# Attention stage of a two-layer trunk on one core: norm and first queries ahead of the values' products, scores with turned sign, small sums moved between engines

## The chip, the core and the metric

The kernel runs on one core of a Trainium2 chip. A core has five engines with a queue of instructions each, worked through in order: TensorE (PE in the rows; its weight loads are PEld) multiplies matrices into PSUM, VectorE (DVE) and ScalarE (ACT) do elementwise work, GpSimd (POOL) too, and SyncE (SP) issues DMA transfers. They meet only at semaphores. The metric is the device time of one execution in microseconds, the median of three runs.

## What is computed

The input is one sequence of 512 tokens with 1024 channels in float32. Layer 0 mixes by causal pooling, layer 1 by attention over a window of 128 tokens; each is followed by a gated MLP with a short convolution. The change touches the attention of layer 1 alone:

```python
qkv = h @ w_qkv + b_qkv                       # h = rms_norm(x, g); 16 query heads, 4 key/value heads of 64
scores = einsum(q, k_band) * 64**-0.5         # 4 blocks of 128 queries, each against 256 keys
scores = where(mask, scores - slope[head] * dist, -inf)
m = maximum(max(scores, -1), sink[head])
p = exp(scores - m)
denom = sum(p, -1) + exp(sink[head] - m)
o = einsum(p / denom, v_band)
return o @ w_o
```

## The kernel before

Activations lie with channels on the partitions: eight tiles `h[c]` of 128 channels by 512 tokens. Every product in float32 is made of three passes (`mm3`, lines 84 to 86): each operand is split into a high and a low part, and high by high, high by low and low by high are added in PSUM. So each 128 by 1024 weight tile takes one ScalarE instruction for the high part (line 98) and one subtraction for the low part (line 99), on VectorE or on GpSimd as the caller says; `proj` asks for GpSimd. The high and low tiles rotate through four buffers, so the split of a tile waits for the last product with the tile four before it; the raw tiles rotate through three.

The RMS norm is folded in late. The products use `h` scaled by the norm's weights only. `norm1.stats` sums squares over channels with four tiny matmuls (line 230), a chain of small VectorE instructions makes the reciprocal root (`rsqrt_mean`, lines 190 to 204), and `norm1.spread` spreads it over the partitions (VectorE line 240, four matmuls line 241, one ScalarE copy, line 244). Keys, queries and values are multiplied by it (`rb`, or `r` per token) when they leave PSUM.

The attention stage starts with three groups of products: keys (`kps`, weight tiles kq0 and kq1, 48 matmuls of 512 columns), values (`vps`, 96 of 256 columns), and the eight query chunks (weight tiles kq2 to kq9, 24 of 512 columns each; chunk c makes `q[c]`). `queries(c, ps)` takes a chunk out of PSUM: a product with `rb` on VectorE (line 451), scale and bias on ScalarE (452), then for each half a copy on ScalarE (458) and a subtraction on VectorE (459). `keys(n)` does the like for a key head.

Then come 16 units, one for each key head n and block b. `scores(n, b)` makes 8 score matmuls of 256 columns (line 540) and four VectorE instructions (543), which add the ALiBi distance and accumulate the row maximum into `neg`; then VectorE turns the sign of `neg` (554) and forms `es` (555), ScalarE takes the exponential of `es` (556) and of the four heads with the row sums (559), VectorE adds the denominator and inverts it (560, 561), and GpSimd scales the four heads (563). Two units later `transposed` turns them (571) and splits them (574, 575), three units later `weighted` multiplies them by the values (12 matmuls of 256 columns) and splits the result into `oh` and `ol` (590, 591).

Between them `fill(upto, have)` puts other TensorE work: one step is three matmuls of 512 columns, first of the remaining query chunks, then of the output projection with `w_o`. `RATE` says how many steps go to one unit. The program's order is what the author writes, but a scheduler below the language may let instructions of one engine pass each other, so the order on each engine is shown from the built program. PSUM has eight banks, here in four rings: t (banks 6, 7), s (2, 3, 4), pj (5, 0) and av (1).

Of the kernel before, what the change touches and what calls it, by code (L numbers as in the profile page):

```python
# [22 lines left out]
AF = mybir.ActivationFunctionType  # L23
# [4 lines left out]
D = 1024  # L28
# [29 lines left out]
def trunk(ctx: ExitStack, tc: tile.TileContext, x_tok, x_t, vecs, w_pool, w_kq, w_v, w_o, w_in, w_out, out_a, out_b):  # L58
# [18 lines left out]
    def bank(tag):  # L77
        rings[tag].append(rings[tag].pop(0))
        return banks[rings[tag][-1]]
# [13 lines left out]
    def weights(src, n, name, eng=None, raw=None):  # L93

        raw = raw or fetch(src, n, name)
        h = wp.tile([P, 1024], F32R, tag="wh", name=f"{name}_h")
        l = wp.tile([P, 1024], F32R, tag="wl", name=f"{name}_l")
        A.activation(h[:, :n], raw[:, :n], AF.Copy)  # L98
        (eng or V).tensor_tensor(l[:, :n], raw[:, :n], h[:, :n].bitcast(F32), ALU.subtract)  # L99
        return h, l  # L100
# [282 lines left out]
    with tc.tile_pool(name="ap", bufs=2) as ap:  # L383
# [16 lines left out]
        for t in (vh, vl):  # L400
            G.memset(t.bitcast(F32), 0.0)

        def proj(i, ps, ks=range(NC), w=None):
            w = w or weights(w_kq[i], D, f"kq{i}", G)
            for k in ks:
                mm3(ps, part(w, k), xs1[k], k == 0, k == NC - 1)
            return w


        qps = bank("pj")  # L410
        vps = [bank("s") for a in range(2)]
        ssp = bank("av")
        kps = [bank("t") for c in range(2)]
        kw = [weights(w_kq[i], D, f"kq{i}") for i in range(2)]
        wv = [weights(w_v[:, a * 1024 : (a + 1) * 1024], 1024, f"wv{a}") for a in range(2)]
        for k in range(NC):
            for c in range(2):
                proj(c, kps[c], [k], kw[c])
        for j in range(NT):
            for k in range(NC):  # L420
                xk = tuple(t[:, j * P : (j + 1) * P] for t in xs1[k])
                wk = part(wv[k // 4], k % 4, 256)
                mm3(vps[j // 2][:, (j % 2) * 256 : (j % 2 + 1) * 256], xk, wk, k == 0, k == NC - 1)
        r = norm1.stats(ssp)
        proj(2, qps)
        rb = norm1.spread(bank("s"), r)

        ku = []
        for c in range(2):
# [32 lines left out]

        key = {0: keys(0)}
        q = {0: queries(0, qps)}
        for j in range(NT):
            ps = vps[j // 2][:, (j % 2) * 256 : (j % 2 + 1) * 256]
            vv = ap.tile([P, 256], F32, tag="vv", name=f"vv{j}", bufs=1)
            V.scalar_tensor_tensor(vv, ps, r[:, j : j + 1], vec[:, V_BV : V_BV + 256], ALU.mult, ALU.add)
            dh, dl = (t[:, j, : 8 * HD].rearrange("p (n z d) -> p n z d", n=4, z=2)[:, :, 1, :] for t in (vh, vl))
            v4 = vv.rearrange("p (n d) -> p n d", n=4)  # L470
            A.activation(dh, v4, AF.Copy)
            V.tensor_tensor(dl, v4, dh.bitcast(F32), ALU.subtract)  # L472
        oh = ap.tile([P, NC, S], F32R, name="oh", bufs=1)
        ol = ap.tile([P, NC, S], F32R, name="ol", bufs=1)

# [24 lines left out]

        def work():

            for c in range(1, NC):
                for _ in fill_q(c):
                    yield 0
            for m, ks in ((0, range(4)), (1, range(4)), (0, range(4, 6)), (1, range(4, 6))):
                yield 2 * ks.stop
                for _ in fill_wo(m, "pj", ks):
                    yield 2 * ks.stop
            for m in range(2, 4):  # L510
                yield NU
                for _ in fill_wo(m, "s", range(6)):
                    yield NU
# [11 lines left out]
        def scores(n, b):  # L525
            w = P if b == 0 else 2 * P
            neg = small(ap, 4, 32, tag="neg", name=f"neg{n}{b}", bufs=3)
            den = small(ap, 4, 16, tag="den", name=f"den{n}{b}", bufs=3)
            es = small(ap, 4, 16, tag="es", name=f"es{n}{b}", bufs=3)
            sink = vec[:, V_SINK + 4 * n : V_SINK + 4 * n + 4]  # L530
            kk = max(b - 1, 0) * P
            sc = []
            for pr in range(2):
                ps = bank("s")
                st = ap.tile([P, 2, 2 * P], F32, tag="sc", name=f"sc{n}{b}{pr}", bufs=6)
                for par in range(2):
                    o = ps[:, par * 256 : par * 256 + 256]
                    qt = q[2 * n + pr][par][:, b * P : (b + 1) * P]
                    for x, kt in enumerate(key[n]):
                        T.matmul(o, lhsT=qt, rhs=kt[:, kk : kk + 256], start=x == 0, stop=x == 1)  # L540
                for par in range(2):
                    i = 2 * pr + par
                    V.tensor_tensor_reduce(  # L543
                        out=st[:, par, :w],
                        in0=ps[:, par * 256 : par * 256 + w],
                        in1=dist[:, 2 * P - w :],
                        scale=slopes[4 * n + i],
                        scalar=sink[:, i : i + 1],
                        op0=ALU.add,
                        op1=ALU.max,  # L550
                        accum_out=neg[:, i : i + 1],
                    )
                sc.append(st)
            V.tensor_scalar(neg, neg, -1.0, None, ALU.mult)
            V.tensor_tensor(es, neg, sink, ALU.add)
            A.activation(es, es, AF.Exp)
            heads = [sc[i // 2][:, i % 2, :w] for i in range(4)]
            for i, t in enumerate(heads):
                A.activation(t, t, AF.Exp, bias=neg[:, i : i + 1], accum_out=den[:, i : i + 1])  # L559
            V.tensor_tensor(den, den, es, ALU.add)  # L560
            V.reciprocal(den, den)
            for i, t in enumerate(heads):
                G.tensor_scalar(t, t, den[:, i : i + 1], 1.0, ALU.mult, ALU.mult)
            return sc
# [26 lines left out]
            V.tensor_tensor(dl, p2, dh.bitcast(F32), ALU.subtract)  # L591


        RATE = 3.4
        fill(2 * NC, 0)
        sc, pt = {}, {}
        for i in range(NU + 3):
            base = 2 * NC + i * RATE
            have = max(i - 3, 0) if i < NU else NU
            if i < NU:  # L600
                n, b = units[i]
                if b == 0:
                    fill((2 * n + 1) * NC, 0)
                sc[i] = scores(n, b)
                if b == 2 and n + 1 < NKV:
                    key[n + 1] = keys(n + 1)
            fill(base + 2 * RATE / 3, have)
            if 0 <= i - 3 < NU:
                weighted(*units[i - 3], pt.pop(i - 3))
                have += 1  # L610
            if 0 <= i - 2 < NU:
                pt[i - 2] = transposed(*units[i - 2], sc.pop(i - 2))
            fill(base + RATE, have)
# [152 lines left out]
```

## Time and profile before

| | |
|---|---|
| median of 3 runs | 944.49 us (944.37 to 944.62) |
| profiled execution, whole | 944.47 us |
| its span, first to last instruction | 942.7 us |
| granted TensorE clock, mean over the span | 0.993 of full speed |
| matmuls busy | 919.2 us (97%) |
| VectorE, ScalarE, GpSimd busy | 62%, 45%, 15% |

The sum in the prediction is made against the profiled execution: 942.7 us of span and 1.8 us around it, 944.47 us, which is the median of the runs within 0.02 us. Busy time of the matmuls counts overlapping instructions once; where the engine starts a matmul of 512 columns every 0.23 us it works without a gap, although each row says 0.39 us. The attention stage runs from about 390 us (first keys' product) to 592 us (end of the output projection).

### The profile page before, as it was taken

The numbers are of one execution on the slowest core, as the hardware profiler recorded it, in microseconds if no ns is written. First come the engines' busy times: TensorE is split into PE (matmuls) and PEld (weight loads), VectorE is DVE, ScalarE is ACT, GpSimd is POOL, SyncE is SP. The second block draws the span as 40 slices with busy tenths as digits, with TensorE's granted clock in tenths as the row PEclk, the third lists the DMA queues.
The fourth block names the chain that finished last, engine by engine and source line by source line (L and its number), as shares of the span: only waits on it lengthen the run. The fifth ranks groups of instructions, "written<-read, shape, count | busy, mean of one in ns | idle before, by whom it ended". The sixth has DMA issues, their size and how long they took to land.

```text
span 942.7 us, 11713 instructions
## 1 busy us (share of the span) xinstructions
PE 919.2 (97%) x4419; PEld 773.1 (82%) x4419; DVE 587.2 (62%) x974; ACT 426.5 (45%) x690; POOL 138.9 (15%) x203
## 2 busy tenths in 40 slices
PE   8999999999999999996999999999999999999997
PEld 7788888888888888885888888888888888888886
DVE  5689775336777654338888581897753367776433
ACT  7565443223444434226877561644432234444432
POOL 9600000000000001442654231000000000000023
PEclk9999999999999999998999999999999999999999
DMA  9133322342322233321101041332223332232312
GB/s 331 64 112 112 111 63 79 98 140 92 112 90 84 75 90 109 112 90 67 46 24 46 1 135 45 112 125 98 65 89 94 133 111 91 90 98 63 92 62 90
DMA packets 28855, 88.13 MB, mean 93 GB/s; under 512 B 3200, under 2 KB 4352, under 8 KB 28800
## 3 DMA queue, kind: packets, MB, share of 16 engines
q1 hardware_dynamic: 28800, 87.40, 28.3%
q8 instruction: 34, 0.56, 0.2%
q14 instruction: 21, 0.17, 0.1%
HBM read 85.29 MB, written 2.10 MB: 93 GB/s over the span
## 4 chain that ended last, share of the span: by engine, by line
PE 90%; DVE 5%; ACT 3%; POOL 1%; issue 1%; ACTq 0%; DVEq 0%; POOLq 0%
PE bank L85 29%; PE bank L84 29%; PE bank L86 29%; PE bank L540 1%; DVE q L459 1%; PE bank L571 1%; ACT sc L559 1%; DVE sc L543 1%; ACT px_h L251 0%; DVE tl L575 0%; DVE vl L472 0%; ACT wi_h L98 0%; PE bank L271 0%; DVE f0x_l L252 0%; PE bank L230 0%
## 5 line engine op out<-in xcount | busy, mean ns | idle before, releaser
L224 POOL TENSOR_TENSOR n_acc<-n_acc,n_sq 128x512 f32<-128x512 f32 (+1 forms) x28 | 39.1, 1397 | 714.2 <-ACT n_sq L215 707.7
L98 ACT ACTIVATE wi_h<-wi_raw 128x1024 fp32r<-128x1024 f32 x88 | 93.0, 1061 | 109.3 <-PE bank L85 102.4
L85 PE MATMUL bank<-f0x_l,wi_h 128*128 128x512 f32 x352 | 137.1, 389 | 0.8 <-DVE f0x_l L252 0.8
L84 PE MATMUL bank<-f0x_h,wi_h 128*128 128x512 f32 x352 | 137.3, 390 | 0.0
L84 PE MATMUL bank<-f1x_h,wi_h 128*128 128x512 f32 x352 | 137.1, 390 | 0.0
L84 PE MATMUL bank<-zh,wo_h 128*128 128x512 f32 (+1 forms) x363 | 137.0, 378 | 0.0
L86 PE MATMUL bank<-f0x_h,wi_l 128*128 128x512 f32 x352 | 137.0, 389 | 0.0
L86 PE MATMUL bank<-f1x_h,wi_l 128*128 128x512 f32 x352 | 137.0, 389 | 0.0
L85 PE MATMUL bank<-f1x_l,wi_h 128*128 128x512 f32 x352 | 136.9, 389 | 0.0
L86 PE MATMUL bank<-zh,wo_l 128*128 128x512 f32 (+1 forms) x363 | 136.6, 376 | 0.0
L85 PE MATMUL bank<-zl,wo_h 128*128 128x512 f32 (+1 forms) x363 | 136.6, 376 | 0.0
L99 DVE TENSOR_TENSOR wi_l<-wi_raw,wi_h 128x1024 fp32r<-128x1024 f32 x84 | 102.8, 1225 | 48.8 <-ACT wi_h L98 36.7
L98 ACT ACTIVATE wo_h<-wo_raw 128x768 fp32r<-128x768 f32 (+1 forms) x70 | 57.5, 822 | 124.0 <-PE bank L85 112.1
L313 DVE TENSOR_TENSOR c_u<-bank,n_rb 128x512 f32<-128x512 f32 x88 | 60.1, 688 | 76.2 <-PE bank L86 76.2
L99 DVE TENSOR_TENSOR wo_l<-wo_raw,wo_h 128x768 fp32r<-128x768 f32 (+1 forms) x66 | 60.4, 915 | 54.4 <-ACT wo_h L98 54.2
L86 PEld LDWEIGHTS bank<-zh,wo_l 128*128 128x128 f32 x363 | 68.3, 188 | 12.5
L84 PEld LDWEIGHTS bank<-zh,wo_h 128*128 128x128 f32 x363 | 68.3, 188 | 12.4
L85 PEld LDWEIGHTS bank<-zl,wo_h 128*128 128x128 f32 x363 | 68.3, 188 | 12.3
L85 PEld LDWEIGHTS bank<-f0x_l,wi_h 128*128 128x128 f32 x352 | 66.1, 188 | 14.7 <-DVE f0x_l L252 1.2
L84 PEld LDWEIGHTS bank<-f0x_h,wi_h 128*128 128x128 f32 x352 | 66.1, 188 | 14.2 <-DVE h L305 0.4
L86 PEld LDWEIGHTS bank<-f1x_h,wi_l 128*128 128x128 f32 x352 | 66.1, 188 | 13.9
L316 ACT ACTIVATE c_t<-c_u,vec 128x512 f32<-128x512 f32 x88 | 70.6, 810 | 15.2 <-DVE c_u L313 14.3
(173 smaller groups left out, 1510.6 us busy)
## 6 DMA issues: line engine op xcount, KB each, us to landing
wi_raw<-w_in SPq DMA_DIRECT2D x88, 512.0 KB, 3.2
wo_raw<-w_out SPq DMA_DIRECT2D x31, 384.0 KB, 3.0
wo_raw<-w_out SPq DMA_DIRECT2D x31, 320.0 KB, 2.9
kq_raw<-w_kq SPq DMA_DIRECT2D x10, 512.0 KB, 3.2
wo_raw<-w_o SPq DMA_DIRECT2D x8, 512.0 KB, 3.3
xt<-x_tok SPq DMA_DIRECT2D x4, 512.0 KB, 5.2
h<-x_t SPq DMA_DIRECT2D x8, 256.0 KB, 7.5
wpool_raw<-w_pool SPq DMA_DIRECT2D x2, 512.0 KB, 8.2
```

The lines of the kernel that those rows point to most:

```text
L84: T.matmul(ps, lhsT=wh, rhs=xh, start=start, stop=False, **kw)
L85: T.matmul(ps, lhsT=wh, rhs=xl, start=False, stop=False, **kw)
L86: T.matmul(ps, lhsT=wl, rhs=xh, start=False, stop=stop, **kw)
L98: A.activation(h[:, :n], raw[:, :n], AF.Copy)
L99: (eng or V).tensor_tensor(l[:, :n], raw[:, :n], h[:, :n].bitcast(F32), ALU.subtract)
L224: eng.tensor_tensor(self.acc[:, lo:hi], self.acc[:, lo:hi], sq[:, lo:hi], ALU.add)
L313: V.tensor_tensor(u, ps, rb, ALU.mult)
L316: A.activation(t, u, AF.Identity, bias=col(V_CB + layer * 2 * NF + m), scale=cw[2])
L459: V.tensor_tensor(t[dst], u[src], t[src].bitcast(F32), ALU.subtract)
L540: T.matmul(o, lhsT=qt, rhs=kt[:, kk : kk + 256], start=x == 0, stop=x == 1)
L543: V.tensor_tensor_reduce(out=st[:, par, :w], in0=ps[:, par * 256 : par * 256 + w], in1=dist[:, 2 * P - w :], scale=slopes[4 * n + i], scal ...
L559: A.activation(t, t, AF.Exp, bias=neg[:, i : i + 1], accum_out=den[:, i : i + 1])
```

## The change

Five edits, all in the attention stage.

1. The sums of the norm and the first query chunk (`q[0]`, weight tile kq2) with the norm's spread now precede the values' products; before, they followed them. The split of kq2 is written ahead of the values' first tile, that of the values' second tile after the spread.
2. The second query chunk (kq3) is projected before the units and taken out of PSUM after the values (`q[1] = queries(1, qps)`); before, the two chunks kq3 and kq4 were filled in as one block ahead of the first scores (`fill(2 * NC, 0)`). That block is gone, `work()` starts at chunk 2, and `RATE` goes from 3.4 to 4 steps per unit, counted from 0.
3. `proj` splits tiles up to kq3 on VectorE instead of GpSimd.
4. The scores carry the opposite sign: negated slopes, negated sinks (`nsink`, made once), minimum in place of maximum, and a scale of -1 in the exponential. The sign turn on VectorE (line 554) falls away.
5. `es` is formed on GpSimd instead of VectorE, and its exponential comes after those of the four heads.

```diff
+        nsink = small(ap, NH, 64, name="nsink", bufs=1)
+        V.tensor_scalar(nsink, vec[:, V_SINK : V_SINK + NH], -1.0, None, ALU.mult)
         def proj(i, ps, ks=range(NC), w=None):
-            w = w or weights(w_kq[i], D, f"kq{i}", G)
+            w = w or weights(w_kq[i], D, f"kq{i}", G if i > 3 else V)
...
-        qps = bank("pj")
-        vps = [bank("s") for a in range(2)]
-        ssp = bank("av")
         kps = [bank("t") for c in range(2)]
         kw = [weights(w_kq[i], D, f"kq{i}") for i in range(2)]
-        wv = [weights(w_v[:, a * 1024 : (a + 1) * 1024], 1024, f"wv{a}") for a in range(2)]
+        w0 = weights(w_kq[2], D, "kq2")
+        wv = [weights(w_v[:, :1024], 1024, "wv0")]
         for k in range(NC):
             for c in range(2):
                 proj(c, kps[c], [k], kw[c])
+        r = norm1.stats(bank("av"))
+        qps = bank("pj")
+        proj(2, qps, w=w0)
+        rb = norm1.spread(bank("s"), r)
+        wv.append(weights(w_v[:, 1024:], 1024, "wv1"))
+        vps = [bank("s") for a in range(2)]
         for j in range(NT):
...
-        r = norm1.stats(ssp)
-        proj(2, qps)
-        rb = norm1.spread(bank("s"), r)
...
         q = {0: queries(0, qps)}
+        qps = bank("pj")
+        proj(3, qps)
...
+        q[1] = queries(1, qps)
...
-            for c in range(1, NC):
+            for c in range(2, NC):
...
-            sink = vec[:, V_SINK + 4 * n : V_SINK + 4 * n + 4]
+            sink = nsink[:, 4 * n : 4 * n + 4]
...
-                        scale=slopes[4 * n + i],
+                        scale=-slopes[4 * n + i],
...
-                        op1=ALU.max,
+                        op1=ALU.min,
...
-            V.tensor_scalar(neg, neg, -1.0, None, ALU.mult)
-            V.tensor_tensor(es, neg, sink, ALU.add)
-            A.activation(es, es, AF.Exp)
+            G.tensor_tensor(es, neg, sink, ALU.subtract)
...
-                A.activation(t, t, AF.Exp, bias=neg[:, i : i + 1], accum_out=den[:, i : i + 1])
+                A.activation(t, t, AF.Exp, bias=neg[:, i : i + 1], scale=-1.0, accum_out=den[:, i : i + 1])
+            A.activation(es, es, AF.Exp)
...
-        RATE = 3.4
-        fill(2 * NC, 0)
+        RATE = 4
...
-            base = 2 * NC + i * RATE
+            base = i * RATE
...
-                    fill((2 * n + 1) * NC, 0)
+                    fill(2 * n * NC, 0)
```

The first place is TensorE from the last keys' product to the first scores. In the names, `kq` and `wv` are weight tiles, `ax` the normed-weight activations, `q0_0` and `q0_1` the two halves of query chunk 0, `kh0` the first key head. Before:

```order
L86 MATMUL bank7_77<-ax7_h_3012,kq1_l_3063 128x512
L84 MATMUL bank2_72<-wv0_h_3068,ax0_h_2642 128x256
...
L230 MATMUL bank1_71<-ones_182,n1_acc_2646 128x2 x4
L84 MATMUL bank5_75<-ax0_h_2642,kq2_h_3246 128x512
...
L241 MATMUL bank4_74<-n1_d_3274,ones_182 128x128 x4
L84 MATMUL bank0_70<-ax0_h_2642,kq3_h_3326 128x512
...
L84 MATMUL bank5_75<-ax0_h_2642,kq4_h_3365 128x512
...
L540 MATMUL bank2_72<-kh0_3291,q0_0_3300 128x256
```

And now:

```order
L86 MATMUL bank7_77<-ax7_h_3012,kq1_l_3065 128x512
L230 MATMUL bank1_71<-ones_182,n1_acc_2646 128x2 x4
L84 MATMUL bank5_75<-ax0_h_2642,kq2_h_3070 128x512
...
L241 MATMUL bank2_72<-n1_d_3174,ones_182 128x128 x4
L84 MATMUL bank3_73<-wv0_h_3076,ax0_h_2642 128x256
...
L84 MATMUL bank0_70<-ax0_h_2642,kq3_h_3310 128x512
...
L548 MATMUL bank2_72<-kh0_3293,q0_0_3302 128x256
...
L84 MATMUL bank5_75<-ax0_h_2642,kq4_h_3396 128x512
...
L548 MATMUL bank3_73<-kh0_3293,q1_0_3357 128x256
```

The norm's sums, the first query chunk and the spread have moved ahead of the 96 values' products, kq3 follows these, and the first scores stand behind kq3; the 24 matmuls of kq4, which stood ahead of the scores, stand among them (`bank5` between the scores of chunk 0 and of chunk 1).

The second place is GpSimd around the first unit of the second key head (n = 1, b = 0). The names are `kq8_l`, the low part of a weight tile, `sc031`, the scores of unit n = 0, b = 3 (second pair of heads), and `es10`, the small sum of unit n = 1, b = 0. Before:

```order
L99 TENSOR_TENSOR kq7_l_3701<-kq7_raw_3698,kq7_h_3700 128x1024
L99 TENSOR_TENSOR kq8_l_3888<-kq8_raw_3885,kq8_h_3887 128x1024
L563 TENSOR_SCALAR sc000_3405<-sc000_3405,den00_3403 128x128 x2
L563 TENSOR_SCALAR sc001_3412<-sc001_3412,den00_3403 128x128 x2
L563 TENSOR_SCALAR sc010_3453<-sc010_3453,den01_3451 128x256 x2
L563 TENSOR_SCALAR sc011_3460<-sc011_3460,den01_3451 128x256 x2
L99 TENSOR_TENSOR kq9_l_4041<-kq9_raw_4038,kq9_h_4040 128x1024
L563 TENSOR_SCALAR sc020_3492<-sc020_3492,den02_3490 128x256 x2
```

And now:

```order
L562 TENSOR_TENSOR es03_3525<-neg03_3523,nsink_3054 128x4
L570 TENSOR_SCALAR sc030_3526<-sc030_3526,den03_3524 128x256 x2
L570 TENSOR_SCALAR sc031_3533<-sc031_3533,den03_3524 128x256 x2
L99 TENSOR_TENSOR kq8_l_3935<-kq8_raw_3932,kq8_h_3934 128x1024
L99 TENSOR_TENSOR kq9_l_4098<-kq9_raw_4095,kq9_h_4097 128x1024
L562 TENSOR_TENSOR es10_3599<-neg10_3597,nsink_3054 128x4
L570 TENSOR_SCALAR sc100_3600<-sc100_3600,den10_3598 128x128 x2
```

Before, kq7 and kq8 were split ahead of the scaling of the first unit's heads and kq9 after the second unit's; now the splits of kq8 and kq9 stand in one block between the scaling of unit n = 0, b = 3 and the small sum of unit n = 1, b = 0.

The third place is VectorE around the splits of query chunk 3, which key head 1 uses. `q3_u` is the chunk out of PSUM, `q3_0` and `q3_1` its halves, `neg` and `es` a unit's row maximum and small sum, `tl` the low part of transposed heads. Before:

```order
L560 TENSOR_TENSOR den02_3490<-den02_3490,es02_3491 128x4
L554 TENSOR_SCALAR neg03_3560<-neg03_3560 128x4
L561 RECIPROCAL den02_3490<-den02_3490 128x4
L459 TENSOR_TENSOR q3_0_3531<-q3_u_3528,q3_0_3531 64x512
L459 TENSOR_TENSOR q3_1_3534<-q3_u_3528,q3_1_3534 64x512
L575 TENSOR_TENSOR tl000_3554<-bank6_76,th000_3553 128x512
L555 TENSOR_TENSOR es03_3562<-neg03_3560,vec_90 128x4
L560 TENSOR_TENSOR den03_3561<-den03_3561,es03_3562 128x4
```

And now:

```order
L582 TENSOR_TENSOR tl010_3574<-bank7_77,th010_3573 128x512
L582 TENSOR_TENSOR tl011_3582<-bank6_76,th011_3581 128x512
L456 TENSOR_TENSOR q3_u_3588<-bank0_70,n1_rb_3183 128x512
L551 ISA sc100_3600,neg10_3597<-bank4_74,dist_3023,nsink_3054 128x128
L551 ISA neg10_3597 128x1
L551 ISA sc100_3600,neg10_3597<-bank4_74,dist_3023,nsink_3054 128x128
L551 ISA neg10_3597 128x1
L464 TENSOR_TENSOR q3_0_3591<-q3_u_3588,q3_0_3591 64x512
L464 TENSOR_TENSOR q3_1_3594<-q3_u_3588,q3_1_3594 64x512
```

The splits of chunk 3 (line 464, before 459) now stand behind the first score instructions of unit n = 1, b = 0; before, they stood a unit earlier, behind the scores of unit n = 0, b = 3. The sign turn (554) and the small sum (555) of each unit are gone from VectorE's queue.

## Rows read from the trace of the kernel before

**Rows 1.** The page: the line of busy time of TensorE's matmuls (share of the span, count), and the chain that ended last, by engine.

```profile
PE 919.2 (97%) x4419; PEld 773.1 (82%) x4419; DVE 587.2 (62%) x974; ACT 426.5 (45%) x690; POOL 138.9 (15%) x203
...
PE 90%; DVE 5%; ACT 3%; POOL 1%; issue 1%; ACTq 0%; DVEq 0%; POOLq 0%
```

**Rows 2.** The view of stretches: us, then busy time with count of PE, PEld, DVE, ACT and POOL, then the granted TensorE clock as a share of full speed, the DMA share and GB/s. The first stretch is the seam before the scores, the second the units of the attention, the third its tail and the output projection.

```profile
426.00:446.00 20.00, 12.44 (x48) 9.84 (x48) 16.37 (x30) 13.51 (x23) 5.11 (x2) 0.83 0.23 79
...
468.00:513.00 45.00, 40.69 (x256) 36.25 (x255) 37.77 (x115) 34.42 (x99) 23.41 (x34) 0.96 0.11 36
...
513.00:592.00 79.00, 79.00 (x412) 67.36 (x411) 42.62 (x89) 35.58 (x80) 18.87 (x24) 1.00 0.16 54
```

**Rows 3.** The view of waits over the whole span, TensorE alone: who waited for whom, us in total, times, longest.

```profile
PE bank L540 <- DVE q L459: 5.2, 3, 2.3
PE bank L84 <- DVE q_u L451: 3.3, 1, 3.3
PE bank L85 <- DVE tl L575: 2.1, 3, 1.4
PE bank L84 <- DVE ol L591: 1.3, 1, 1.3
```

**Rows 4.** TensorE's timeline from the values' products to the second unit's scores: start, us, line, operation, and in brackets how long the engine sat idle before and what ended it.

```profile
401.20 0.28 PE L84 MATMUL bank<-wv_h,ax_h 128*128 128x256 f32 x1
...
412.72 0.95 PE L230 MATMUL bank<-ones,n_acc 128*128 128x2 f32 x8
...
419.58 1.16 PE L241 MATMUL bank<-n_d,ones 128*128 128x128 f32 x8 [0.32 <-DVE n_d L240]
...
425.82 0.39 PE L86 MATMUL bank<-ax_h,kq_l 128*128 128x512 f32 x1
...
429.48 0.47 PE L84 MATMUL bank<-ax_h,kq_h 128*128 128x512 f32 x1 [3.26 <-DVE q_u L451]
...
434.81 0.39 PE L86 MATMUL bank<-ax_h,kq_l 128*128 128x512 f32 x1
...
437.93 0.51 PE L540 MATMUL bank<-kh,q 128*128 128x256 f32 x1 [2.26 <-DVE q L459]
...
440.68 0.58 PE L540 MATMUL bank<-kh,q 128*128 128x256 f32 x1 [2.03 <-DVE q L459]
...
441.27 0.63 PE L84 MATMUL bank<-ax_h,kq_h 128*128 128x512 f32 x1
...
445.47 0.40 PE L86 MATMUL bank<-ax_h,kq_l 128*128 128x512 f32 x1
```

**Rows 5.** GpSimd's timeline: splits of weights, two instructions in a row in each of these rows.

```profile
412.66 4.75 POOL L99 TENSOR_TENSOR kq_l<-kq_raw,kq_h 128x1024 fp32r<-128x1024 f32 x2 [6.20 <-ACT kq_h L98]
...
434.97 5.11 POOL L99 TENSOR_TENSOR kq_l<-kq_raw,kq_h 128x1024 fp32r<-128x1024 f32 x2 [9.02 <-PE bank L85]
```

**Rows 6.** VectorE's timeline, same columns: two steps of the norm's small chain; two splits of a query chunk, the product that takes the next chunk out of PSUM, and two splits later on; a unit's small sum and its sign turn where they took long.

```profile
413.90 1.17 DVE L192 TENSOR_SCALAR rs_i<-rs_v 128x4 int32<-128x4 int32 x1
415.11 2.32 DVE L193 TENSOR_SCALAR rs_y<-rs_i 128x4 int32<-128x4 int32 x1
...
435.44 5.18 DVE L459 TENSOR_TENSOR q<-q_u,q 64x512 fp32r<-64x512 f32 x2 [1.22 <-ACT q L458]
440.66 0.69 DVE L451 TENSOR_TENSOR q_u<-bank,n_rb 128x512 f32<-128x512 f32 x1
...
442.89 1.41 DVE L459 TENSOR_TENSOR q<-q_u,q 64x512 fp32r<-64x512 f32 x2 [0.26 <-ACT q L458]
...
463.39 1.85 DVE L555 TENSOR_TENSOR es<-neg,vec 128x4 f32<-128x4 f32 x1
...
506.13 1.94 DVE L554 TENSOR_SCALAR neg<-neg 128x4 f32<-128x4 f32 x1
```

**Rows 7.** TensorE's timeline in the units: three products or scores that waited, and eight transposes in two places.

```profile
470.61 0.38 PE L85 MATMUL bank<-tl,vh 128*128 128x256 f32 x1 [1.37 <-DVE tl L575]
...
491.10 0.35 PE L84 MATMUL bank<-th,vh 128*128 128x256 f32 x1 [1.27 <-DVE ol L591]
...
494.03 1.91 PE L571 MATMUL bank<-ident,sc 128*128 128x128 f32 x8
...
505.24 1.03 PE L571 MATMUL bank<-ident,sc 128*128 128x128 f32 x8
...
512.48 0.39 PE L540 MATMUL bank<-kh,q 128*128 128x256 f32 x1 [0.91 <-DVE q L459]
```

**Rows 8.** ScalarE's timeline: the bias of a query chunk, its two splits, and the load of the table for the exponentials.

```profile
441.38 0.82 ACT L452 ACTIVATE q_u<-q_u,bqs,qs 128x512 f32<-128x512 f32 x1 [4.24 <-DVE q_u L451]
442.23 1.28 ACT L458 ACTIVATE q<-q_u 64x512 fp32r<-64x512 f32 x2
443.53 1.28 ACT L559 ACT_TABLE_LOAD   x1
```

**Rows 9.** Groups. VectorE's small sum over the 16 units (columns: busy us, mean ns of one, idle time before). Then lines of the view by source line (ns min/median/max, first and last start): GpSimd's four small two-operand instructions at the program's start, and the splits of key and query weights, on GpSimd and on VectorE.

```profile
L555 DVE TENSOR_TENSOR es<-neg,vec 128x4 f32<-128x4 f32 x16 | 5.1, 320 | 0.2
...
L172 POOL TENSOR_TENSOR band<-band,ident x4: 198/214/671, 3.7 to 7.2; 128x1 f32<-128x1 f32 x1, 128x3 f32<-128x3 f32 x1, 128x7 f32<-128x7 f32 x1, 128x15 f32<-128x15 f32 x1
...
L99 POOL TENSOR_TENSOR kq_l<-kq_raw,kq_h x8: 2364/2404/2792, 401.7 to 453.2; 128x1024 fp32r<-128x1024 f32 x8
...
L99 DVE TENSOR_TENSOR kq_l<-kq_raw,kq_h x2: 1224/1225/1226, 380.6 to 384.0; 128x1024 fp32r<-128x1024 f32 x2
```

## The prediction

> **What bounds the kernel now.** I read the page first. TensorE's matmuls are busy 97% of the span and the chain that ended last lies on TensorE for 90% [rows 1]. So work taken off another engine is worth only what TensorE waited for it, and the question is where the missing 3% lie. The view of waits answers: nearly all of TensorE's waits are in the attention, on splits of queries (5.2 us), on one product that takes queries out of PSUM (3.3 us), and on splits of transposed and weighted heads (2.1 and 1.3 us) [rows 3]. The view of stretches then says which stage: 7.6 us idle at the seam ahead of the scores, with a granted clock of 0.83; 4.3 us idle in the units, clock 0.96; nothing in the tail up to the output projection's end [rows 2]. Beyond 513 us there is nothing to win.
>
> The seam in order of time [rows 4]: values' products from 401.20 to 412.72, 96 matmuls, 0.12 us each; norm's sums; chunk 0; a wait of 0.32 us for the spread; chunk 1 until 426.05 (the last start plus one step of 0.23 us). Then TensorE has run out of what needs no norm. It waits 3.26 us for a bank, does chunk 2 (24 matmuls, 5.56 us from 429.48), starts the scores and waits 2.26 and 2.03 us for the two halves of chunk 1; the next matmuls run at the lower of the clock's two levels, 1.2 GHz (0.63 instead of 0.39 us). From 426.05 to 445.70 pass 19.65 us, in which TensorE does 24 matmuls (5.56), 8 scores (8 x 0.12 = 0.96) and 12 matmuls (12 x 0.23 = 2.78), 9.30 us in all. **The seam loses 10.35 us**, with the spread's wait 10.7 us.
>
> Why VectorE is late there: while GpSimd splits two weight tiles in a row, VectorE's small chain takes 1.17 and 2.32 us for steps on four numbers, and two query splits take 5.18 us together, against 1.41 us for two later on [rows 5, 6]. A VectorE instruction of this kind ends only when GpSimd's ends.
>
> The units lose 4.3 us in waits (2.1 + 1.3 + the 0.91 of rows 7) and, at clock 0.96 over 45 us, up to 45 x 0.04 = 1.8 us more: eight transposes take 1.91 us after a wait and 1.03 us elsewhere [rows 2, 3, 7]. **The units lose 6.1 us.** Everything else being pure TensorE work that the change does not alter, the whole prize is 10.7 + 6.1 = 16.8 us.
>
> **The change, part by part.**
>
> *Norm and chunk 0 ahead of the values.* TensorE now goes keys, sums, chunk 0, spread, 96 value products (11.52 us), chunk 1 (5.56 us), first scores. The spread's chain has chunk 0's 5.56 us as cover; the two slow steps, 3.49 us now, should become small ones, but two weight splits on VectorE (1.22 us each [rows 9]) stand between them. With 13 small steps at an estimated 0.2 us that is 2.4 + 2.6 = 5.0 us, with 0.32 us each (the mean of the small sums [rows 9]) 6.6: it about fits; I allow 0.1 us of wait (0 to 1.0). Behind the spread, everything that made TensorE wait (copy, keys, chunk 0's halves) has 11.52 + 5.56 = 17 us of cover, while now the stretch from the spread at 419.58 to the first scores behind 434.81 is 15.4 us with all its stalls. So the 3.26 us go. If the cover failed by 3 us, they would be back.
>
> *Chunk 1 and the scores.* What is late next are the halves of chunk 1. By the order, TensorE has behind chunk 1's last matmul 4 scores, 12 matmuls, 4 scores and 5 matmuls: 0.48 + 2.78 + 0.48 + 1.16 = 4.9 us. The path: the product 0.69 on VectorE, the bias 0.82, the table load 1.28 and a first exponential (about 0.5, an estimate from the small ScalarE rows) which now stand ahead of the split, the split 0.64, VectorE's half 0.70, some 0.6 us for a weight split of ScalarE's ahead and handovers [rows 6, 8]: 5.2 us. Wait 0.3 for the first half, 0.35 for the second: **0.65 us**. The ends are 0 and the 4.3 us of now plus the slow clock behind them, 12 matmuls in 4.43 instead of 2.78 us, 1.65; I take the low value because only one GpSimd split (2.40 us [rows 9]) falls here and ends before the halves come.
>
> *First weight splits on VectorE.* kq2 and kq3 cost VectorE 1.22 us each in place of GpSimd's 2.40 us [rows 9], while it has little to do. They cost nothing beyond the chain above.
>
> *No sign turn, small sum on GpSimd.* VectorE loses 16 small sums (5.1 us [rows 9]) and as many sign turns of about that size; two of these were held up 1.85 and 1.94 us behind a GpSimd split [rows 6]. GpSimd gains 16 instructions; the nearest rows are its four small two-operand ones, 0.2 to 0.67 us [rows 9], so 3 to 11 us on an engine busy 23.41 of 45 us [rows 2]. None of this is TensorE's time by itself; it shortens the way from scores to transposes. Its bound is the units' 4.3 us of waits, most on VectorE's queue, and zero.
>
> The Trainium skill speaks against this edit: "Perfetto Trace Analysis", section Optimizing Scalar/DVE Operations, says that VectorE and GpSimd share a read port, so that moving work between the two might not help. By the rows two blocked instructions of nearly 2 us leave VectorE's queue; by the page their waits come back on GpSimd's. The sum below gives the units 0.5 us; by the page that would be nothing, 934.5 us instead of 934.1.
>
> *RATE 4 without the block of 16 steps.* A query chunk pair is now finished just when its key head's first unit comes, where before it was a unit ahead. For head 1 the order shows the price: on GpSimd two splits stand in a row (kq8, kq9), the pattern that cost 5.18 us at 435.44 [rows 5, 6], and the halves of chunk 3 come on VectorE while they run. TensorE's cover from chunk 3's last matmul to its first score is 4 scores, 9 matmuls, 12 products, 8 transposes and 2 matmuls: 0.48 + 2.07 + 1.44 + 0.8 + 0.46 = 5.25 us. The second split ends 2 x 2.40 us after the first begins, and that begins, by my estimate, 3 us after the last matmul (ScalarE has heads and a key to copy first): 7.8 us, so a wait of 2.6, with the second half **2.8 us** (0 to the 4.3 of now). Of the four waits of over 1.2 us two were followed by the lower clock, those at 437.93 and 491.10, and two were not, 429.48 and 470.61 [rows 4, 7]; the longer wait on splits was: **1.6 us** (0 to 1.65). Heads 2 and 3 have one split in that place; the present 0.91 us [rows 7] is the upper end for each: **0.5 us** together. The first transposed heads stand on ScalarE behind three units' exponentials: **0.7 us** (0 to 1.37, the present wait [rows 7]).
>
> *Sum.* Seam: 10.7 - 0.1 - 0.65 = 9.95 us gained. Units: 6.1 - 2.8 - 1.6 - 0.5 - 0.7 = 0.5 us gained. Together 10.4 us; the profiled execution, 944.47 us, stands 0.02 from the median: **934.1 us**.
>
> **The rivals.**
>
> *The seam's wait comes back at chunk 1.* For it: the table load and a weight split stand ahead of the halves, and GpSimd splits kq5 to kq7 in this stretch. Against: kq7's split begins right after chunk 1's last matmul and is over before the halves come. Price 4.3 + 1.65 in place of 0.65: 5.3 us, 939.4 us.
>
> *The units run free too.* If chunk 3's halves slip in ahead of the second split, neither its wait nor the clock's drop comes: 934.1 - 2.8 - 1.6 - 0.5 = 929.2 us. For it: VectorE is some 10 us lighter, and each unit has 12 instead of 10.2 matmuls as cover. Against: the order of GpSimd.
>
> *Slower: GpSimd's queue holds ScalarE.* ScalarE's exponential of `es` now waits for an instruction that stands on GpSimd behind the scaling of the unit before and, in six units, a 2.40 us split; behind it wait the denominator on VectorE and the transposes' splits on ScalarE. ScalarE is busy 34.42 of 45 us [rows 2], so some 10 us per 45, 22 us over the 16 units, are free. A wait w per unit costs 16w - 22; it eats the 10.4 us from w = 2.0. With a split's 2.40 us in every unit: 38 - 22 - 10.4 = 6 us slower, 950 us. Against: the sum is ready while the four exponentials, 2 us, still run.
>
> *No change.* The values' evacuation (eight VectorE instructions) stands ahead of chunk 1's in the queue; if it were late as a whole, the seam's wait would only change its name: 944 us.
>
> **How the numbers follow.** Forecast 0.57, chunk 1's wait 0.14, free units 0.20, slower 0.05, no change 0.04. The best known bound is 944.47 - 16.8 = 927.7 us; free units give 929.2, the first rival 939.4. The range 929 to 940 us leaves out the two last cases and the outer part of the others, 2 in 10. Faster by over 0.2% (1.9 us, about what a measurement of this kernel can tell from no change): 0.57 + 0.14 + 0.20 = 0.91; within: 0.04; slower: 0.05.
>
> **What would show it.** Right: in the profile after, no wait of over 1 us between the keys' products and the first scores, the clock full there, the 3.26 us gone; one wait of 2 to 3 us at the first scores of chunk 3, with GpSimd's two splits over it. Wrong: a wait at chunk 1's halves of over 2 us; exponentials of `es` that ScalarE waits for in most units; or no wait at chunk 3.

## The result

The changed kernel took 932.41 us (median of 4 runs, 930.72 to 932.51), the kernel before 944.43 us beside it (944.01 to 944.62): ratio 0.9869, interval 0.9852 to 0.9886. The profiled execution took 932.39 us, of which the span is 930.6, 12.1 us less than before.

The stretches of the profile after, in the order that [rows 2] uses (stretch in us, its length, busy time and number of instructions of TensorE, of its weight loads, of VectorE, ScalarE and GpSimd, then the granted clock, the DMA share and GB/s):

```profile
413.00:426.00 13.00, 13.00 (x89) 12.04 (x88) 8.60 (x14) 7.37 (x12) 4.95 (x2) 1.00 0.20 64
426.00:446.00 20.00, 19.56 (x110) 16.49 (x109) 14.51 (x53) 17.64 (x51) 11.29 (x21) 1.00 0.14 51
446.00:468.00 22.00, 19.14 (x118) 17.07 (x117) 15.66 (x47) 16.90 (x47) 12.87 (x18) 0.92 0.22 73
468.00:513.00 45.00, 44.34 (x291) 39.82 (x290) 34.01 (x116) 36.10 (x108) 24.01 (x45) 1.00 0.10 36
```

The stretch from 426 to 446, which was 12.44 of 20 us busy at clock 0.83, is now 19.56 busy at 1.00. The one poor stretch is from 446 to 468: 2.86 us idle, clock 0.92. TensorE's waits in the attention have shrunk from four kinds to two [rows 3] (columns: us in total, times, longest):

```profile
PE bank L548 <- DVE q L464: 3.4, 2, 2.9
...
PE bank L85 <- DVE tl L582: 0.4, 1, 0.4
```

TensorE's timeline after, beside [rows 4]: norm's sums, spread (no wait), first scores, the scores on chunk 1's two halves (no wait, and 0.13 us of a gap), then chunk 3's.

```profile
401.15 0.95 PE L230 MATMUL bank<-ones,n_acc 128*128 128x2 f32 x8
...
407.55 1.05 PE L241 MATMUL bank<-n_d,ones 128*128 128x128 f32 x8
...
425.42 0.28 PE L548 MATMUL bank<-kh,q 128*128 128x256 f32 x1
...
430.27 0.38 PE L548 MATMUL bank<-kh,q 128*128 128x256 f32 x1
...
430.73 0.28 PE L548 MATMUL bank<-kl,q 128*128 128x256 f32 x1
430.98 0.39 PE L548 MATMUL bank<-kh,q 128*128 128x256 f32 x1
...
451.64 0.38 PE L548 MATMUL bank<-kh,q 128*128 128x256 f32 x1 [2.86 <-DVE q L464]
...
452.36 0.58 PE L548 MATMUL bank<-kh,q 128*128 128x256 f32 x1
...
455.09 0.63 PE L85 MATMUL bank<-ax_l,kq_h 128*128 128x512 f32 x1
...
455.80 0.40 PE L84 MATMUL bank<-ax_h,kq_h 128*128 128x512 f32 x1
...
475.86 0.39 PE L548 MATMUL bank<-kh,q 128*128 128x256 f32 x1 [0.58 <-DVE q L464]
```

The wait of 2.86 us is followed by matmuls at 1.2 GHz (0.63 us instead of 0.40) until about 455.5. What stood over it is in the timelines of GpSimd and of VectorE (beside [rows 5, 6]):

```profile
446.34 4.70 POOL L99 TENSOR_TENSOR kq_l<-kq_raw,kq_h 128x1024 fp32r<-128x1024 f32 x2 [0.19 <-ACT kq_h L98]
```

```profile
402.14 0.16 DVE L190 TENSOR_SCALAR rs_v<-bank 128x4 f32<-128x4 f32 x1 [7.17 <-PE bank L230]
...
404.56 0.16 DVE L193 TENSOR_SCALAR rs_y<-rs_i 128x4 int32<-128x4 int32 x1
...
406.33 0.16 DVE L204 SCALAR_TENSOR_TENSOR n_r<-rs_t,rs_y 128x4 f32<-128x4 f32 x1
...
448.85 3.45 DVE L464 TENSOR_TENSOR q<-q_u,q 64x512 fp32r<-64x512 f32 x2 [2.09 <-ACT q L463]
...
463.72 1.41 DVE L464 TENSOR_TENSOR q<-q_u,q 64x512 fp32r<-64x512 f32 x2 [0.28 <-ACT q L463]
```

Splits of kq8 and kq9 run in a row from 446.34 to 451.04; chunk 3's halves, whose copies ScalarE finished at 448.85, end at 452.30, while those of chunk 4 take 1.41 us together. The norm's steps that took 1.17 and 2.32 us [rows 6] take 0.16.

### The profile page after: what moved, and what is told of

It reads as the page before. It is cut to its first block, busy times and chain, and to the rows that moved or that the text cites. A ratio compares the mean times of both kernels' runs of the same rounds, so it can differ in the third digit from the quotient of the medians.

```text
span 930.6 us, 11682 instructions
## 1 busy us (share of the span) xinstructions
PE 915.2 (98%) x4419; PEld 771.5 (83%) x4419; DVE 574.8 (62%) x945; ACT 427.3 (46%) x690; POOL 135.1 (15%) x217
## 4 chain that ended last, share of the span: by engine, by line
PE 92%; ACT 3%; DVE 2%; POOL 2%; issue 1%; POOLq 0%; ACTq 0%
PE bank L84 30%; PE bank L85 30%; PE bank L86 30%; PE bank L548 1%; PE bank L578 1%; ACT sc L565 1%; DVE q L464 1%; ACT px_h L251 0%; POOL sc L570 0%; PE bank L241 0%; ACT q_u L457 0%; DVE sc L551 0%; ACT wi_h L98 0%; PE bank L271 0%; ACT th L581 0%
```

## The experiments

Twelve kernels ran, four on each of three chips. The kernel before spread from 939.0 to 945.5 us over those runs, so the kernels are set beside the changed one's 932.41 us by their medians (two edits that turned out to do next to nothing gave 932.06 and 933.07 there, so differences of under 0.7 us are not read as effects), and the ratio to before is given where before is what counts.

**What each part does.** e1_front_only: the new order and RATE 4, and nothing else of the change.

```
-            w = w or weights(w_kq[i], D, f"kq{i}", G if i > 3 else V)
+            w = w or weights(w_kq[i], D, f"kq{i}", G)
...
-            G.tensor_tensor(es, neg, sink, ALU.subtract)
+            V.tensor_scalar(neg, neg, -1.0, None, ALU.mult)
+            V.tensor_tensor(es, neg, sink, ALU.add)
+            A.activation(es, es, AF.Exp)
```

> The new order of norm, chunk 0, values and chunk 1 and RATE 4, with the sign turn, the small sum on VectorE and the splits of kq2 and kq3 on GpSimd as before. Theory (the order of the seam carries the gain, the small sums about 0.5 us): 932.5 to 934.5 us, no wait of over 1 us between the keys' products and the first scores; the wait at chunk 3's halves stays at 2 to 3 us. Rival (VectorE's relief carries a good part, since its small steps stood behind GpSimd's splits): 936 us or more, with waits of 1 us and more at the spread or at chunk 1's halves.

939.43 us (938.19 to 941.87, 12 runs), 0.9971 of before [0.9954, 0.9987]. The stretches of its profile, the seam and the units:

```profile
426.00:446.00 20.00, 19.07 (x107) 15.91 (x106) 15.56 (x57) 16.52 (x48) 7.49 (x13) 1.00 0.17 53
...
468.00:513.00 45.00, 39.07 (x243) 34.24 (x242) 34.61 (x113) 34.38 (x104) 19.71 (x31) 0.96 0.11 36
```

The order of the seam did its work (TensorE is busy for 19.07 of 20 us), but the units lost more than before: 39.07 of 45 us busy, clock 0.96. By the number the rival is right, by the places it is not: the spread costs 0.38 us and chunk 1's halves 0.78. The long waits are for the halves of chunk 3 and of later chunks (1.78, 2.01 and 1.95 us) and for a weighted head (1.38 us). Two pairs of these halves take 3.24 and 3.15 us beside a GpSimd split, the collision that e11_sign_turn shows below.

e2_signs_only: before with the sign turned and the small sum on GpSimd, no new order.

> The kernel before with the turned sign and the small sum on GpSimd alone. Theory: TensorE is short of nothing that these take away; the waits at the seam stand, and the units give back between 0 and 2 us of their 4.3: 942.5 to 944.5 us. Rival (VectorE's queue of small sums is what holds the units): over 3 us faster, 941.5 us or less. Rival of the other sign (GpSimd's queue holds ScalarE's exponential): 945.5 us or more.

943.56 us, ratio 1.0012 [0.9996, 1.0028]: nothing, as the theory has it. The seam's three waits stand (3.27, 2.26 and 1.96 us). The units did change, in two ways that cancel: from 446 to 513 us TensorE idles 5.72 us instead of 4.31, and the clock from 468 on is 1.00 instead of 0.96.

e3_splits_gpsimd: `G if i > 3 else V` and the explicit kq2 back to GpSimd.

> The changed kernel with the splits of kq2 and kq3 back on GpSimd. Theory (VectorE's small steps stand behind GpSimd's splits): if a split of 2.40 us falls over the norm's chain, one or two of its steps take up to 2.3 us instead of 0.16, and TensorE waits up to 3 us for the spread: 932.5 to 936 us. Rival (the chain has cover enough, since the splits come earlier or chunk 0's 5.56 us hide it): 932.2 to 932.6 us.

933.07 us (932.87 to 934.05): 0.66 us over the changed kernel, in the theory's range, near its lower end. A wait of 0.38 us for the spread's operand has come back; the rest is not read as an effect. Against e1_front_only, which differs from this kernel by the small edits alone (the sign, the sums' engine and the place of their exponential), these are worth 6.4 us in the new order. No run has the place of the exponential alone.

e11_sign_turn: the changed kernel, with VectorE's turn of the sign again (and maxima for minima), the sum on GpSimd.

```
-            G.tensor_tensor(es, neg, sink, ALU.subtract)
+            V.tensor_scalar(neg, neg, -1.0, None, ALU.mult)
+            G.tensor_tensor(es, neg, sink, ALU.add)
```

> The changed kernel with the sign turned by an instruction of VectorE's again (16 small ones), the sum on GpSimd behind it. Theory (of TensorE's time this is worth what it makes ScalarE's exponentials late): 0 to 2 us slower than the changed kernel, 932.4 to 934.5 us. Rival (the turn behind GpSimd's splits is what cost the 6.4 us between the runs with and without both small edits): 936 to 939 us, with steps of the turn of 1 to 2 us and waits for halves or heads in the later units.

937.45 us: 5.04 us slower, in the rival's range (the profiled run took 938.93). But the turn is not slow, as the rival had it: it takes 0.16 to 0.17 us in every unit. What has changed is where GpSimd's splits of the output weights fall. In this kernel's timelines of GpSimd, VectorE and TensorE, three of the four now begin just as a chunk's halves do:

```profile
463.60 2.40 POOL L99 TENSOR_TENSOR wo_l<-wo_raw,wo_h 128x1024 fp32r<-128x1024 f32 x1
...
476.86 2.36 POOL L99 TENSOR_TENSOR wo_l<-wo_raw,wo_h 128x1024 fp32r<-128x1024 f32 x1 [0.32 <-ACT wo_h L98]
...
502.66 2.36 POOL L99 TENSOR_TENSOR wo_l<-wo_raw,wo_h 128x1024 fp32r<-128x1024 f32 x1 [0.52 <-ACT wo_h L98]
```

```profile
463.99 3.26 DVE L461 TENSOR_TENSOR q<-q_u,q 64x512 fp32r<-64x512 f32 x2
...
477.33 3.15 DVE L461 TENSOR_TENSOR q<-q_u,q 64x512 fp32r<-64x512 f32 x2 [1.06 <-ACT q L460]
...
503.13 3.16 DVE L461 TENSOR_TENSOR q<-q_u,q 64x512 fp32r<-64x512 f32 x2 [0.39 <-ACT q L460]
```

```profile
479.81 0.52 PE L545 MATMUL bank<-kh,q 128*128 128x256 f32 x1 [2.01 <-DVE q L461]
...
505.62 0.39 PE L545 MATMUL bank<-kh,q 128*128 128x256 f32 x1 [1.73 <-DVE q L461]
```

These three pairs of halves take 3.15 to 3.26 us, and TensorE waits 2.01 and 1.73 us for two of them, besides 1.78 us for those of chunk 3 and 1.20 for a weighted head. In the changed kernel the four splits of the output weights begin at 461.42, 472.86, 485.32 and 496.21 us and end 0.1 to 0.4 us after the halves begin (463.72, 474.91, 487.62, 498.35), which take 1.41 to 1.62 us. This is read from the traces: no run turns the sign on VectorE and holds the splits in place.

**The wait at chunk 3.** Three kernels were to take away a cause each. e5_kq9_dve and e6_kq89_dve move one split or both to VectorE; e7_rate_ahead starts the fill steps four earlier.

```
-            w = w or weights(w_kq[i], D, f"kq{i}", G if i > 3 else V)
+            w = w or weights(w_kq[i], D, f"kq{i}", G if 3 < i < 9 else V)
```

```
-            base = i * RATE
+            base = 4 + i * RATE
```

In e6_kq89_dve the bounds are `3 < i < 8`.

> The changed kernel with the split of kq9 on VectorE, ahead of chunk 3's halves there; TensorE's and ScalarE's order is the same. Theory (two GpSimd splits in a row hold chunk 3's halves, and this wait lowers the clock): the halves take 0.7 to 1.5 us each instead of 3.45, the wait of 2.86 us falls to under 1.3, and the stretch at 1.2 GHz behind it goes or shrinks: 928 to 931 us. Rival (ScalarE's queue ahead of the halves, or the chunk's being just in time, sets the wait): the wait stays at 2 us or more, 932 to 933.5 us.

> The changed kernel with the splits of kq8 and kq9 on VectorE. Theory (GpSimd's split over the halves is what counts): VectorE has two splits of about 1.2 us ahead of the halves, which then take 0.7 us each: wait 0 to 1 us, 928 to 930.5 us. Rival (VectorE is the queue that is late there): two more splits in it make the wait longer than with one of them moved, 931 to 934 us.

> The changed kernel with the fill steps four steps ahead in all units (about a third of a query chunk). Theory (the place of GpSimd's splits against chunk 3's halves sets the wait): the chunk comes some 2.8 us earlier, the splits too, so a part of the wait goes, at most its 2.86 us; but other places get fewer matmuls as cover: 929 to 933.5 us, and two splits still stand in a row. Rival (the just-in-time rate alone sets the wait): the wait at chunk 3 goes whole, with halves still as slow, 928 to 930 us.

930.16, 928.87 and 928.39 us. The timeline of VectorE in e5_kq9_dve shows the halves free of the split, and late all the same, since the one on VectorE, itself held up while GpSimd does kq8, stands ahead of them:

```profile
447.23 2.59 DVE L99 TENSOR_TENSOR kq_l<-kq_raw,kq_h 128x1024 fp32r<-128x1024 f32 x1 [0.47 <-ACT kq_h L98]
449.85 1.40 DVE L464 TENSOR_TENSOR q<-q_u,q 64x512 fp32r<-64x512 f32 x2
```

So a wait of 1.80 us stays, more than the 1.3 expected, but the clock stays at 1.00 behind it in this profile (929.93 us); two of the five runs, 931.10 and 931.47 us, had the changed kernel's mean clock of 0.996. With both on VectorE (e6_kq89_dve) the two splits take 2.36 us, and the halves begin a little later than in the changed kernel, free of any split (timelines of VectorE and TensorE):

```profile
449.03 1.40 DVE L464 TENSOR_TENSOR q<-q_u,q 64x512 fp32r<-64x512 f32 x2
```

```profile
449.77 0.39 PE L548 MATMUL bank<-kh,q 128*128 128x256 f32 x1 [0.68 <-DVE q L464]
```

This is the cleanest of the three: nearly the same start, no GpSimd split, and the wait falls from 2.86 to 0.68 us. So of the 2.86 us some 2 are the split's (3.45 us less 1.40) and the rest is the halves' start, which there waited for ScalarE's copies. In e7_rate_ahead the pair on GpSimd is parted, against the expectation, and the halves stand over its second split:

```profile
434.08 2.40 POOL L99 TENSOR_TENSOR kq_l<-kq_raw,kq_h 128x1024 fp32r<-128x1024 f32 x1 [1.54 <-ACT kq_h L98]
...
443.62 2.39 POOL L99 TENSOR_TENSOR kq_l<-kq_raw,kq_h 128x1024 fp32r<-128x1024 f32 x1
```

```profile
444.44 2.84 DVE L464 TENSOR_TENSOR q<-q_u,q 64x512 fp32r<-64x512 f32 x2
```

TensorE waits 0.70 and 0.22 us for them. The rival's time came out, but not its reason: the earlier start and the parted pair are not told apart here. All three beat the changed kernel.

e4_es_dve: the small sum on VectorE in every unit, the sign still turned. e10_es_dve_late: the same in the 12 units behind key head 0 alone.

```
-            G.tensor_tensor(es, neg, sink, ALU.subtract)
+            (G if n == 0 else V).tensor_tensor(es, neg, sink, ALU.subtract)
```

> The changed kernel with the small sum of every unit on VectorE (the sign stays turned). Theory (the engine of this sum is not TensorE's business): within 0.7 us of the changed kernel, 931.8 to 933.2 us. Rival (the two engines share what they wait for, and GpSimd was the right place): 1 us or more slower, with steps of 1 to 2 us for this sum behind GpSimd's splits. Rival (GpSimd's queue held ScalarE): 1 us or more faster.

> The changed kernel with the small sum on VectorE in the 12 units behind key head 0 and on GpSimd in its first four. With the sum on VectorE in all units GpSimd's splits of kq8 and kq9 stand apart (four scalings and three more units' worth between them); here they stand in a row as in the changed kernel. Theory (what the kernel with all sums on VectorE gained, 3.7 us, is that place): 931.5 to 932.8 us, the wait of 2.5 to 3 us at chunk 3's halves there again. Rival (the engine of the sums is what gained): three quarters of it stay, 929 to 930 us.

928.76 us (928.68 to 928.82) and 932.06 us. The first refuted the theory as it was written: 3.65 us faster. The second shows that it was not the sums' engine: twelve of the sixteen sums on VectorE gained 0.35 us, and in e10_es_dve_late the pair of splits, the held halves and the wait at chunk 3 are all there still (GpSimd's timeline, VectorE's, TensorE's waits):

```profile
446.35 4.70 POOL L99 TENSOR_TENSOR kq_l<-kq_raw,kq_h 128x1024 fp32r<-128x1024 f32 x2 [0.18 <-ACT kq_h L98]
```

```profile
448.86 3.46 DVE L464 TENSOR_TENSOR q<-q_u,q 64x512 fp32r<-64x512 f32 x2 [2.08 <-ACT q L463]
```

```profile
PE bank L548 <- DVE q L464: 3.4, 2, 2.9
```

With the sums of the first four units there too, kq8 and kq9 no longer stand in a row on GpSimd (its timeline in e4_es_dve):

```profile
435.98 2.40 POOL L99 TENSOR_TENSOR kq_l<-kq_raw,kq_h 128x1024 fp32r<-128x1024 f32 x1 [0.23 <-ACT kq_h L98]
...
450.36 2.39 POOL L99 TENSOR_TENSOR kq_l<-kq_raw,kq_h 128x1024 fp32r<-128x1024 f32 x1 [3.91 <-ACT kq_h L98]
```

Chunk 3's halves lie between them, at 447.65, 1.2 us earlier than in the changed kernel, and take 1.40 us; TensorE waits for no chunk before 472.63 (0.93 us). VectorE's timeline there also shows which of its work a split holds:

```profile
450.54 0.35 DVE L551 CUSTOM_DVE_ANT_0 sc<-bank,dist,nsink 128x128 f32<-128x128 f32 x1
450.81 0.08 DVE L551 DVE_READ_ACCUMULATOR2_ANT neg<- 128x1 f32 x1
450.81 0.69 DVE L582 TENSOR_TENSOR tl<-bank,th 128x512 fp32r<-128x512 f32 x1
451.42 1.35 DVE L562 TENSOR_TENSOR es<-neg,nsink 128x4 f32<-128x4 f32 x1
```

While GpSimd splits from 450.36 to 452.75, the scores and a `tl`, which read PSUM and one tile of SBUF, take their usual time. The small sum, which reads two tiles of SBUF, ends with the split. Two tiles are not needed for that: the steps of [rows 6] that took 1.17, 2.32 and 1.94 us beside a split read one tile, of SBUF.

**The pace.** e9_pace_before: the changed kernel with the pace of before.

```
-        RATE = 4
+        RATE = 3.4
+        fill(NC, 0)
...
-            base = i * RATE
+            base = NC + i * RATE
```

> The changed kernel with the pace of before: a whole block of 8 steps (chunk 2) ahead of the units, RATE 3.4. GpSimd's kq8 is split with kq4 to kq7 before the units, kq9 alone later. Theory (two splits in a row over chunk 3's halves cost the 2.86 us and the clock behind it): no wait over 1 us there, 928 to 930 us. Rival (the new pace is itself a gain of the change, since the old one leaves the later units too few matmuls): waits in the later units of 2 us and more, 932 to 936 us.

935.11 us: the rival's range, though by the theory's mechanism in another place. Chunk 3 waits no more, kq9's split now falls on a denominator, and `tl` is queued behind that on VectorE (timelines of GpSimd, VectorE and TensorE):

```profile
443.09 2.38 POOL L99 TENSOR_TENSOR kq_l<-kq_raw,kq_h 128x1024 fp32r<-128x1024 f32 x1 [0.19 <-POOL es L562]
```

```profile
443.18 2.32 DVE L567 TENSOR_TENSOR den<-den,es 128x4 f32<-128x4 f32 x1 [1.47 <-ACT es L566]
```

```profile
447.20 0.39 PE L85 MATMUL bank<-tl,vh 128*128 128x256 f32 x1 [2.44 <-DVE tl L582]
```

The lower clock follows (0.92 from 446 to 468 us), and later waits of 1.30, 1.00 and 1.23 us.

**The slower rival.** e8_es_held makes GpSimd's sum late by 20 small steps in each unit.

```
             G.tensor_tensor(es, neg, sink, ALU.subtract)
+            for _ in range(20):
+                G.tensor_scalar(es, es, 1.0, None, ALU.mult)
```

> The changed kernel with 20 more small steps (times one) on GpSimd behind the small sum of each unit, so that the sum comes some 4 us later and GpSimd has some 64 us more to do over the 16 units. By the price in the prediction (16 w - 22 us, w the time that ScalarE waits per unit, some 2 us of the delay hidden by the four exponentials): w about 2, 10 us slower, 938 to 950 us. If ScalarE's order lets it do other work first, w stays under 1 and the time within 3 us: 932 to 935.5 us.

1001.61 us, ratio to before 1.0614 [1.0592, 1.0636]. ScalarE's waits, first in the changed kernel, then here:

```profile
ACT es L566 <- POOL es L562: 1.4, 4, 0.5
```

```profile
ACT es L568 <- POOL es L564: 74.0, 16, 6.6
```

So w is 74.0 / 16 = 4.6 us, more than twice the expected 2, for the steps, 223 ns each, hold GpSimd for 71.2 us, and its scalings and splits as well. The prediction's price for that w is 16 x 4.6 - 22 = 52 us; 69.2 were paid. The clock, 0.79 to 0.83 in the units, is a part that the price leaves out; how much of the difference it makes is not shown. The mechanism is real; in the changed kernel it costs nothing that can be seen.

**The best.** e12_both joins the sums on VectorE with the earlier fill steps.

> The changed kernel with the small sum on VectorE and the fill steps four steps ahead, both of which left no long wait at chunk 3. Theory: what is left of the prize by then is under 1 us (927.7 us is all of it), so 927.7 to 928.6 us, no better than the better of the two (928.39) by more than 0.7. Rival (one undoes the other's order): 929 us or more.

928.73 us: no better than the better of the two, and just above the expected range. What is left are waits of 0.92 and 0.21 us at chunk 3 and 0.47 us at the output projection.

## Why the prediction was right

The time, 932.41 us, lies 1.7 us under the forecast of 934.1. By the forecast's own losses, with the row of the profile after:

| loss | forecast, us | measured, us |
|---|---|---|
| wait for the spread | 0.1 | 0 |
| chunk 1's halves | 0.65 | 0.13 (gap at 430.98) |
| chunk 3's halves | 2.8 | 2.86 |
| lower clock behind them | 1.6 | 1.8 (22 us x 0.08) |
| later chunks | 0.5 | 0.58 |
| transposed heads | 0.7 | 0.44 |
| sum | 6.35 | 5.8 |

- **The seam.** The 3.26 us wait and chunk 1's two are gone. e1_front_only shows that this is the order's work: with nothing else of the change the stretch from 426 to 446 us is busy for 19.07 of 20 us.
- **Chunk 1's halves** are the term that was mis-sized, 0.5 us too dear. They begin at 429.52 and take 1.40 us together, and no split stands over them; the first score on them starts 4.8 us after chunk 1's last matmul (425.42 to 430.27), where the sum had 5.2.
- **The prize** was counted too small. e7_rate_ahead took 928.39 us with 1.39 us of waits left in the attention (0.70, 0.22 and 0.47); without these it would be at 927.0, an estimate, so before lost at least 17.4 us there instead of 16.8. That and the half microsecond of losses are 1.15 of the 1.7 us; the rest is not told from the rows. (TensorE's work of the stage, from the first keys' product to the end of the output projection, went from 179.5 to 167.1 us; that end is at 569.8 us before, not at 592.)
- **The lower clock** came as forecast, but that was luck in part: the prediction chose between two cases that had followed waits in the kernel before, and one of the changed kernel's four runs seems to have gone without it (930.72 us, mean clock 0.998). It also counted four waits of over 1.2 us where there are five: the one of 2.03 us at 440.68 [rows 3, 4] is missing.
- **Chunk 3** went as told: two GpSimd splits in a row, both halves ending behind the second. That their place is the cause is shown: e10_es_dve_late keeps the pair and the 2.85 us wait, and e6_kq89_dve, with the halves as late as in the changed kernel but no split over them, has 0.68 us left. e4_es_dve parts the pair and loses the wait whole, its halves beginning 1.2 us earlier as well. The rival "the units run free too" (929.2 us) was the price of just that, and e4, e6 and e7 came to 928.4 to 928.9.
- **The small sums** are where the reasoning fell short. The prediction held that the turned sign and the sum's engine were small, for "None of this is TensorE's time by itself". In the old order they are that: 0 in e2_signs_only. But in the new order the turned sign is worth 5.0 us and the sum on GpSimd costs 3.65 us, both by the places that GpSimd's splits then take against the query halves. The new order without them and without edit 3 (e1_front_only) is 7.0 us slower than the changed kernel, so the seam's order alone does not bring the 9.95 of 10.4 us that the prediction's sum gives it. The forecast came out because it took those places from the order of the changed kernel; its reason for giving this edit little was wrong.
- **The Trainium skill's objection.** "Perfetto Trace Analysis", section Optimizing Scalar/DVE Operations, of the Trainium skill says that moving work between VectorE and GpSimd might not help, as they share a read port. The time came out its way, 3.65 us lost by the move to GpSimd, but by a detour: the sums themselves lost nothing that e10_es_dve_late can tell, the place of a weight split did. The Trainium skill's page "SBUF — State Buffer", section SBUF: two separate sides, says that whichever of the two engines starts first locks the shared ports for its whole instruction, and that on VectorE's side this concerns operations with two SBUF inputs or in a two-port mode. The trace of e4_es_dve agrees on the inputs (0.35 and 0.69 us beside a split with one tile of SBUF and PSUM, 1.35 us with two tiles of SBUF); whether the held steps with one SBUF tile in [rows 6] ran in such a mode no run here shows.

## What to carry to other kernels

Where GpSimd runs long operations, list what VectorE does in the same microseconds: a short VectorE step that reads SBUF alone costs what is left of GpSimd's, and this is worth a wait only if TensorE's next operand is that step's or is queued behind it. In a planned order an edit of 0.2 us can move a 2.4 us split onto or off such a step, so price an edit from the order that results, not from the instruction, and undo parts one at a time inside the new order: here their effects did not add (the small edits: 0 in the old order and 6.4 us in the new; there, the sign alone 5.0 us gained, the sums' engine alone 3.65 lost). Where TensorE is the bound, count first what it waits: four kernels came to 928.4 to 928.9 us and none passed it.

## What the runs showed of the hardware

- A small VectorE step that reads SBUF alone ended only with the GpSimd split beside it: 2.32 us for 128x4 numbers, with two inputs (e9_pace_before) and with one [rows 6], against 0.16 without a split. Steps that read PSUM were not held (0.35 and 0.69 us, e4_es_dve).
- Waits of one length were followed by different clocks. A wait of 1.78 us at chunk 3 left the clock from 446 to 468 us at 1.00 in e1_front_only and at 0.92 in e11_sign_turn; one of 1.80 us in e5_kq9_dve left it at 1.00. The changed kernel's own fourth run, 930.72 us, had a mean clock of 0.998 where the others had 0.996 and 932.4 us. So the 1.8 us behind a wait is not certain to be paid in each run.
